# Two edits in a two-layer trunk kernel: the order of the second half's join at the inner norms, and the last held products in two halves of 256 columns

## The chip, the cores and the metric

The kernel runs on one core of one Trainium2 chip. The metric is the device time of one execution in microseconds; the time before is the median of three runs. Five engines work side by side and meet through semaphores: TensorE (PE in the profile, with its weight loads on a row of their own, PEld), VectorE (DVE), ScalarE (ACT), GpSimd (POOL) and SyncE (SP), which issues most DMAs. Each engine works through its own queue of instructions in order.

## The reference

The model has two layers over 256 tokens of 1024 features. Each layer is three steps, each followed by a layer norm over the features:

```python
for l in range(DEPTH):
    h = _swiglu(x, ffn_w1[l, 0], ffn_w3[l, 0], ffn_w2[l, 0])
    x = _layernorm(ALPHA * x + 0.5 * h, ln_g[l, 0], ln_b[l, 0])
    h = _mixer(x, l, ...)
    x = _layernorm(ALPHA * x + h, ln_g[l, 1], ln_b[l, 1])
    h = _swiglu(x, ffn_w1[l, 1], ffn_w3[l, 1], ffn_w2[l, 1])
    x = _layernorm(ALPHA * x + 0.5 * h, ln_g[l, 2], ln_b[l, 2])
return x
```

`_swiglu` is `(silu(x @ w1) * (x @ w3)) @ w2` with 2816 hidden features. `_mixer` projects x to seven parts, runs a gated spatial unit and a differential attention on them, merges both with sigmoid gates and multiplies by `w_out`. `_layernorm` subtracts the mean, divides by the root of the variance plus a small constant, and applies a gain and a bias. All data are float32.

## The kernel before, in words

**Products in three terms.** Every float32 operand of a large product is split into a hi part (the value rounded to the fast float32 format) and a lo part (the rest). A product is three: hi by hi, hi by lo and lo by hi (`three`, line 271). The hi parts are made by ScalarE, the lo parts by VectorE, which subtracts. For weights that is `stream` (lines 174 and 178) or, for the pieces that are loaded ahead of a norm, `ahead` and `rest_of` (207, 216, 227, 229). For activations it is `split` (233 for hi, 234 for lo). Weights are loaded by SP as `raw` tiles of 1 MB through a ring of four.

**Tokens in two row tiles.** The 256 tokens are two tiles of 128, t = 0 and t = 1. At the end of a step a row tile lies with its tokens on the partitions and its 1024 features in two halves of 512 columns; `x_tok[t]` holds it. The next step wants x with the features on the partitions, so it has to be turned.

**The inner norms (class `Norm`).** There are five: three behind an FFN and two behind a mixer. For each row tile, `part_s` (545) adds a half's products and sums the rows. `finish_s` takes the mean (551), then the sum of squares on ScalarE (553), the reciprocal root by three Newton steps on VectorE (`rsqrt`, 243 to 249), and the normalized rows (556), the second 512 columns first. `send` puts these second 512 columns into two planes of 16 bits (184) and has a DMA turn them (`turning`, 189). `turned` is a task that calls `turn(t, 0)` and `turn(t, 1)` after set numbers of beats; a beat is a count of products that TensorE has been given.

- `turn(t, 0)`: TensorE transposes the first 512 columns (633) into a bank; ScalarE applies gain and bias in four pieces of 128 (638), and `split` makes the hi part (ScalarE, 233) and the lo part (VectorE, 234).
- `turn(t, 1)`: ScalarE joins the two planes that the DMA has turned (628, "the join"); then 638, 233 and 234 as before.

The `part_s` of row tile 1 is queued behind the lo part of row tile 0's first half where that has been traced already.

**What sets the order.** TensorE's instructions stand in the order in which they are traced. On the other engines a scheduler at compile time sets each queue's order, by priority and by the times that it reckons. `soon()` gives the instructions in it a higher priority; `behind(ins)` puts each instruction traced in it behind `ins` in the queue of the engine that both use, and does nothing if `ins` is None. The join is in a `soon()` and has no `behind`.

**After a norm.** `gemm_b2` multiplies the turned x by the next weights, first for row tile 0 and then for row tile 1. For row tile 0 the first 512 columns (four blocks of 128) meet two matrices with three products each, and then the second 512.

**The end of an FFN.** `ffn` makes its last product in several pieces: products by a seven-product scheme (S banks), "plain pairs", and the last four pairs of blocks, which are held (`HELD` = 4) until the rest is done. The held products go bank by bank: for t and the column half c, 4 x 2 x 3 = 24 products 512 columns wide into `ends[t, c]`. For the last norm of the kernel, `part` then adds the bank to the rows (567), takes statistics in groups of 256 columns (572) and, at row tile 1, multiplies a part that does not reach the last column by the gain (574). At (t, c) = (1, 1) it is called twice, for 256 columns each, after the last of the 24 products. `finish` gathers the statistics (579), takes the root (583), has TensorE bring the first 768 columns of row tile 1 into banks and subtract the mean times the gain (588 and 592), ends the rows (594 to 600) and stores them in three cuts (601).

Of the kernel before, what the change touches and what calls it, by code (L numbers as in the profile page):

```python
# [17 lines left out]
ALU = mybir.AluOpType  # L18
# [4 lines left out]
T = 256  # L23
NT = T // P
# [9 lines left out]
PQ = [(k, k + 1) for k in (0, 2, *range(FB + 2 * NS, FT, 2))]  # L34
HELD = 4
# [23 lines left out]
def trunk(ctx, tc, x, xT, w13a, w13b, w2s, w2p, wb, wqk, wa, wbr, wo, gateb, sgug, sgub, sguwT, sgubias, lam, diffg,  # L59
          lng, lnb, lngT, lnbT, cosT, sinT, out):  # L60
    nc = tc.nc
    V, A, G, PE = nc.vector, nc.scalar, nc.gpsimd, nc.tensor
# [19 lines left out]
    def bank():  # L82
        return psum.tile([P, 512], F32, tag="main", name=name("bank"))
# [34 lines left out]
    @contextmanager  # L118
    def soon():
        was = tc.cur_priority  # L120
        tc.cur_priority = max(0, was - 2 * STEP)
        yield
        tc.cur_priority = was
# [27 lines left out]
    def behind(ins):  # L151

        return tc.issue_after(ins) if ins is not None else nullcontext()
# [158 lines left out]
    def rows_p(ps, t, q, piece, xh, xl, c0=0, n=512, stop=False, start=False):  # L312

        for j, k in enumerate(q):
            wh, wl = (v[:, j * 512 + c0 : j * 512 + c0 + n] for v in piece)
            three(ps[:, :n], xh(k)[:, t * P : (t + 1) * P], xl(k)[:, t * P : (t + 1) * P], wh, wl,
                  start and j == 0, stop and j == 1)
        beat(n / 1024)
# [190 lines left out]
    class Norm:  # L509
# [5 lines left out]

        def __init__(self, l, i, scale, eps, after, last=False):
            self.scale, self.eps, self.last, self.done = scale, eps, last, set()
            self.ends, self.xlo, self.pre, self.sent = [None] * NT, {}, None, {}
            self.gT, self.bT = (v[:, l, i] for v in (ln_g, ln_b))
            self.y = x_tok  # L520
            self.group = 256 if last else 512
            self.st = [sm("st", D // self.group * 6, bufs=2) for _ in range(NT)]
            self.g, self.b = bc_load(lng[l, i], after), bc_load(lnb[l, i], after)
            if last:
                A.activation(self.g, self.g, AF.Copy, scale=-0.5)
                self.minus = s512("minus")
                A.activation(self.minus[:, :P], ident, AF.Copy, scale=-1.0)
                self.eps_t = self.minus[:, 2 * P : 2 * P + 1]
                V.memset(self.eps_t, eps)
                with behind(silu[0]):  # L530
                    A.activation(sm("first", 1), mask[:, :1], AF.Sqrt)
            else:
                self.x = [xs.tile([P, 4, 512], F32R, tag="x", name=name("x")) for _ in range(2)]
# [88 lines left out]
        def turn(self, t, h):  # L622
            self.done.add((t, h))
            xf = s512("xf")
            if h:
                b = xf
                with soon():
                    A.activation(xf.bitcast(U16).rearrange("p (k w) -> p k w", w=2),
                                 self.sent[t].rearrange("p (w k) -> p k w", w=2), AF.Copy)
            else:  # L630
                b = side_bank()
                for k in range(4):
                    PE.transpose(b[:, k * P : (k + 1) * P], self.y[t][:, k * P : (k + 1) * P], ident)
            hi, lo = (self.x[h][:, :, o + t * P : o + (t + 1) * P] for o in (0, T))
            with soon(), behind(early[0] if t == 0 else None):
                for k in range(4):
                    s, f = slice(k * P, (k + 1) * P), slice(h * 4 + k, h * 4 + k + 1)
                    A.activation(xf[:, s], b[:, s], AF.Identity, scale=self.gT[:, f], bias=self.bT[:, f])  # L638
                with behind((None, self.ends[1])[h] if t == 0 else None):
                    last = split(hi, lo, xf.rearrange("p (k t) -> p k t", k=4))  # L640
            self.xlo[t, h] = last[1]
            if (t, h) == (1, 1):
                latest[:] = last

# [6 lines left out]
    def ffn(l, f, i, norm, following=None):  # L651
# [108 lines left out]
            ln.pre = ahead(following)  # L760
        for t in range(NT):
            for c in range(2):
                for ps, o, n in ends[t, c]:
                    for q in PQ[-HELD:]:
                        rows_p(ps, t, q, held[q, c], hh, hl, o, n, stop=q == PQ[-1])
                    if not last:
                        ln.part_s(t, c, ps)
                        continue
                    for o in ((0, 256) if last and (t, c) == (1, 1) else (0,)):
                        ln.part(t, c * 512 + o, ps[:, o : o + 256] if o or last and (t, c) == (1, 1) else ps, 1.0)  # L770
            (ln.finish if last else ln.finish_s)(t, ((2, 1.5), (2, 1))[t])
            if t == 0:
                with behind(ln.ends[0]):
                    ln.more(1, 0, S[7], ALU.subtract, ln.scale)
                    ln.more(1, 0, u, ALU.add)
                    ln.more(1, 1, v, ALU.add, ln.scale)
                    ln.more(1, 1, S[7], ALU.add)
# [323 lines left out]
```

## Time and profile before

| what | value |
|---|---|
| median of three runs | 1212.53 us (1212.32 to 1212.62) |
| the profiled execution's own time | 1213.05 us |
| its span, from the first to the last instruction | 1211.3 us |
| TensorE's share of the chain that ended last | 91% |
| VectorE's and ScalarE's shares of that chain | 4% and 3% |
| mean granted clock of TensorE | 1.000 |

In the timeline each row has the start and the duration in us, the engine, the line, the operation, the tiles written and read, and in brackets how long the engine had been idle and what ended that. Several instructions in a row of one kind are merged, with their count behind an x. In the list of waits the columns are the total, the number of waits and the longest. The chain that ended last has start, duration and what ran.

### The profile page before, as it was taken

What the parts mean: (1) busy time and instruction counts of PE and PEld (TensorE: products, weight loads), DVE (VectorE), ACT (ScalarE), POOL (GpSimd) and SP (SyncE); (2) the same over time, 40 slices, a digit from 0 to 9 for tenths busy, and PEclk for the clock granted to TensorE, in tenths of its full rate; (3) what the DMA queues carried; (4) which work ended last, traced back from release to release, by engine and by line L of the source; (5) the groups of instructions that cost most, each with busy time, mean ns of one, the idle gap of its engine ahead of it and who ended that gap; (6) DMA issues with size and microseconds to landing.
All of it is one profiled execution on the core that took longest, in us unless ns stands there. A gap on an engine that the chain in (4) does not pass through costs nothing.

```text
span 1211.3 us, 16542 instructions
## 1 busy us (share of the span) xinstructions
PE 1203.7 (99%) x5961; PEld 1011.3 (83%) x5961; DVE 942.9 (78%) x1540; ACT 857.4 (71%) x1384; POOL 91.1 (8%) x184
## 2 busy tenths in 40 slices
PE   9999999999999999999999999999999999999998
PEld 8888888888888878888888888888888888888886
DVE  6658998885696876579985679989766877757797
ACT  7677677679865595776776776776898556867761
POOL 0100000233300000000000000003331000000000
PEclk9999999999999999999999999999999999999999
DMA  8985665655764658665668665766648456677551
GB/s 321 323 261 174 211 249 208 227 177 166 232 227 164 217 178 282 191 192 218 229 216 270 195 176 207 254 223 199 213 139 273 176 174 217 201 259 210 184 202 47
DMA packets 101346, 257.00 MB, mean 212 GB/s; under 512 B 66528, under 2 KB 67600, under 8 KB 74640
## 3 DMA queue, kind: packets, MB, share of 16 engines
q1 hardware_dynamic: 97296, 243.03, 59.9%
q0 software_dynamic: 3536, 12.13, 3.2%
q8 instruction: 46, 0.75, 0.3%
q10 hardware_dynamic: 432, 0.79, 0.2%
q14 instruction: 36, 0.29, 0.1%
HBM read 235.47 MB, written 1.05 MB: 195 GB/s over the span
## 4 chain that ended last, share of the span: by engine, by line
PE 91%; DVE 4%; ACT 3%; issue 1%; DMA 0%; SPq 0%; POOL 0%; DVEq 0%; ACTq 0%; POOLq 0%
PE bank L271 35%; PE sbank L271 24%; PE bank L283 16%; PE bank L290 8%; PE sbank L283 2%; PE bank L446 2%; PE sbank L290 1%; PE sbank L829 1%; DVE wlo L178 1%; PE sbank L961 1%; ACT pp L839 0%; DVE nwa L248 0%; ACT xf L638 0%; ACT whi L174 0%; PE sbank L878 0%
## 5 line engine op out<-in xcount | busy, mean ns | idle before, releaser
L178 DVE TENSOR_TENSOR wlo<-raw,whi 128x1024 fp32r<-128x1024 f32 (+1 forms) x396 | 436.6, 1125 | 144.5 <-ACT whi L174 113.9
L174 ACT ACTIVATE whi<-raw 128x1024 fp32r<-128x1024 f32 (+1 forms) x396 | 372.9, 971 | 124.4 <-PE bank L283 43.2
L271 PE MATMUL bank<-whi,x 128*128 128x512 f32 x840 | 263.3, 390 | 0.0
L271 PEld LDWEIGHTS bank<-whi,x 128*128 128x128 f32 x840 | 157.7, 188 | 32.9 <-DVE gz L293 0.2
L271 PE MATMUL bank<-wlo,x 128*128 128x512 f32 x420 | 163.5, 389 | 0.0
L271 PE MATMUL sbank<-whi,x 128*128 128x512 f32 x512 | 158.9, 389 | 0.0
L283 PE MATMUL bank<-x,whi 128*128 128x512 f32 x640 | 156.0, 394 | 0.0
L283 PEld LDWEIGHTS bank<-x,whi 128*128 128x128 f32 x640 | 117.1, 188 | 26.3 <-issue 2.3
L271 PEld LDWEIGHTS sbank<-whi,x 128*128 128x128 f32 x512 | 96.1, 188 | 20.0
L353 ACT ACTIVATE shi<-raw 128x1024 fp32r<-128x1024 f32 (+1 forms) x80 | 73.4, 946 | 51.7 <-DVE raw L368 26.4
L271 PE MATMUL sbank<-wlo,x 128*128 128x512 f32 x256 | 99.6, 389 | 0.0
L355 DVE TENSOR_TENSOR slo<-raw,shi 128x1024 fp32r<-128x1024 f32 (+1 forms) x80 | 85.4, 1088 | 14.1 <-ACT shi L353 13.3
L271 PEld LDWEIGHTS bank<-wlo,x 128*128 128x128 f32 x420 | 78.9, 188 | 16.0
L290 PE MATMUL bank<-x,wlo 128*128 128x256 f32 x640 | 85.9, 285 | 0.0
L290 PEld LDWEIGHTS bank<-x,wlo 128*128 128x128 f32 x640 | 81.6, 191 | 2.2
L291 ACT ACTIVATE r<-bank 128x256 f32<-128x256 f32 x112 | 41.6, 377 | 24.0 <-PE bank L290 24.0
L271 PEld LDWEIGHTS sbank<-wlo,x 128*128 128x128 f32 x256 | 48.1, 188 | 9.9
L271 PE MATMUL sbank<-whi,hhi 128*128 128x512 f32 x144 | 56.3, 391 | 0.0
L271 PE MATMUL sbank<-whi,hlo 128*128 128x512 f32 x144 | 56.1, 390 | 0.0
L271 PE MATMUL sbank<-wlo,hhi 128*128 128x512 f32 x144 | 56.0, 389 | 0.0
L506 POOL DMA_DIRECT2D bc<-in_lng x6 | 3.2, 530 | 696.2 <-DVE bc L505 696.2
L702 ACT ACTIVATE planes<-silu 128x1024 uint16<-128x1024 uint16 x40 | 42.0, 1053 | 7.3 <-DVE silu L701 6.2
(247 smaller groups left out, 1999.1 us busy)
## 6 DMA issues: line engine op xcount, KB each, us to landing
raw<-in_w13b SPq DMA_DIRECT2D x76, 1024.0 KB, 5.4
raw<-in_w2p SPq DMA_DIRECT2D x24, 1024.0 KB, 4.9
raw<-in_wa SPq DMA_DIRECT2D x24, 1024.0 KB, 5.4
raw<-in_w2s SPq DMA_DIRECT2D x20, 1024.0 KB, 4.9
raw<-in_wb SPq DMA_DIRECT2D x16, 1024.0 KB, 5.3
raw<-in_wqk SPq DMA_DIRECT2D x16, 1024.0 KB, 4.8
raw<-in_wbr SPq DMA_DIRECT2D x16, 1024.0 KB, 4.9
raw<-in_w13a SPq DMA_DIRECT2D x8, 1024.0 KB, 4.8
```

The source lines that it names most:

```text
L174: copied = A.activation(h, r, AF.Copy)
L178: V.tensor_tensor(out=w, in0=r, in1=h.bitcast(F32), op=ALU.subtract)
L271: PE.matmul(ps, xx, w, start=start and n == 0, stop=stop and n == 2)
L283: PE.matmul(b[-1], hi[:, k * P : (k + 1) * P], xc(k), start=k == 0, stop=False)
L290: PE.matmul(b[n][:, :T], lo[:, k * P : (k + 1) * P], xc(k)[:, :T], start=False, stop=k == KT - 1)
L291: emptied[0] = A.activation(r[:, s], b[n][:, T:], AF.Copy, scale=scale).ins
L353: A.activation(h, r, AF.Copy)
L355: V.tensor_tensor(out=w, in0=r, in1=h.bitcast(F32), op=ALU.subtract)
L446: PE.matmul(ps[t][m], x[:, j, o + t * P : o + (t + 1) * P], y, start=k0 + j == 0 and o == 0 and y is hi, stop=k0 + j == KT - 1 and y is lo)
L702: A.activation(pk.rearrange("p (w k) -> p w k", w=2), s.bitcast(U16).rearrange("p (k w) -> p w k", w=2), AF.Copy)
L829: PE.matmul(banks[m][:, j * nk : (j + 1) * nk], rows(qT, m, j, t * P, P), rows(kT, m, j, 0, nk), start=True, stop=True)
L961: PE.matmul(b[:, j * T + t * P : j * T + (t + 1) * P], vg[t][:, g // 4, s], wsT[g // 4][:, s], start=True, stop=True)
```

## The change

At row tile t the hi part's instruction of `turn(t, 0)` is kept in `xhi[t]`, and the join of `turn(t, 1)` is queued behind it on ScalarE. At the last norm, for (t, c) = (1, 1) alone, the held products are done in two halves. The 24 of the left half write columns 0 to 255 of the bank that also holds the sums so far of all 512 columns. Then `part` is called for them, and the old sums in the bank's columns 256 to 511 are added to the rows. The 24 of the right half go to a new bank, which they start from nothing, and `part` adds that to the rows. For all other t and c the products and calls stay what they were.

```diff
             self.scale, self.eps, self.last, self.done = scale, eps, last, set()
-            self.ends, self.xlo, self.pre, self.sent = [None] * NT, {}, None, {}
+            self.ends, self.xlo, self.pre, self.sent, self.xhi = [None] * NT, {}, None, {}, {}
...
             xf = s512("xf")
             if h:
                 b = xf
-                with soon():
+                with soon(), behind(self.xhi[t]):
                     A.activation(xf.bitcast(U16).rearrange("p (k w) -> p k w", w=2),
                                  self.sent[t].rearrange("p (w k) -> p k w", w=2), AF.Copy)
...
                     last = split(hi, lo, xf.rearrange("p (k t) -> p k t", k=4))
-            self.xlo[t, h] = last[1]
+            self.xhi[t], self.xlo[t, h] = last
...
         for t in range(NT):
             for c in range(2):
-                for ps, o, n in ends[t, c]:
-                    for q in PQ[-HELD:]:
-                        rows_p(ps, t, q, held[q, c], hh, hl, o, n, stop=q == PQ[-1])
-                    if not last:
-                        ln.part_s(t, c, ps)
-                        continue
-                    for o in ((0, 256) if last and (t, c) == (1, 1) else (0,)):
-                        ln.part(t, c * 512 + o, ps[:, o : o + 256] if o or last and (t, c) == (1, 1) else ps, 1.0)
+                (ps, _, _), = ends[t, c]
+                if last and (t, c) == (1, 1):
+                    y, right = ln.y[t][:, 768:], bank()
+                    for b, o, opens in ((ps, 0, False), (right, 256, True)):
+                        for q in PQ[-HELD:]:
+                            rows_p(b[:, :T], t, q, held[q, c], hh, hl, o, 256, stop=q == PQ[-1],
+                                   start=opens and q == PQ[-HELD])
+                        ln.part(t, 512 + o, b[:, :T], 1.0)
+                        if not opens:
+                            V.tensor_tensor(out=y, in0=y, in1=ps[:, T:], op=ALU.add)
+                    continue
+                for q in PQ[-HELD:]:
+                    rows_p(ps, t, q, held[q, c], hh, hl, 0, 512, stop=q == PQ[-1])
+                if last:
+                    ln.part(t, c * 512, ps, 1.0)
+                else:
+                    ln.part_s(t, c, ps)
```

## The prediction

> **What bounds the kernel now.** First the head of the page. Its first row has the span, and the row of busy times says how much of it is not matrix products.
>
> ```profile
> span 1211.3 us, 16542 instructions
> ```
> ```profile
> PE 1203.7 (99%) x5961; PEld 1011.3 (83%) x5961; DVE 942.9 (78%) x1540; ACT 857.4 (71%) x1384; POOL 91.1 (8%) x184
> ```
>
> TensorE (PE) is busy for 1203.7 of 1211.3 us. An edit that takes no products away can only win back holes between them and the tail behind the last one. So the second view is the list of waits, for TensorE alone. Two of its rows belong to the inner norms:
>
> ```profile
> PE sbank L633 <- DVE xtok L556: 0.8, 2, 0.4
> PE bank L271 <- DVE x L234: 0.5, 3, 0.2
> ```
>
> L234 writes the lo part of the turned x, which the next layer multiplies by. L556 writes the normalized rows, which TensorE transposes at L633. The idle times listed are smaller than the holes in the order of starts, so I measured the holes there. There are two kinds of norm: three follow an FFN, two a mixer. I show one of each; the others of a kind repeat them to some hundredths. Behind an FFN, in the timeline, ScalarE (ACT) first:
>
> ```profile
> 780.44 1.19 ACT L628 ACTIVATE xf<-sent 128x1024 uint16<-128x1024 uint16 x1
> 781.51 0.64 ACT L233 ACTIVATE x<-xf 128x512 fp32r<-128x512 f32 x1
> 782.04 1.65 ACT L638 ACTIVATE xf<-xf,ln_b,ln_g 128x128 f32<-128x128 f32 x4
> 783.58 0.63 ACT L174 ACTIVATE whi<-raw 128x512 fp32r<-128x512 f32 x1
> 784.10 0.63 ACT L233 ACTIVATE x<-xf 128x512 fp32r<-128x512 f32 x1
> 784.62 1.14 ACT L553 ACTIVATE sq<-xtok,mv 128x1024 bf16<-128x1024 f32 x1
> ```
>
> L628 at 780.44 is the join of the second 512 columns of row tile 0. It stands ahead of L233 at 781.51, the hi part of the first 512 columns, which TensorE needs first. VectorE (DVE) in the same stretch:
>
> ```profile
> 781.77 0.69 DVE L178 TENSOR_TENSOR wlo<-raw,whi 128x512 fp32r<-128x512 f32 x1
> 782.37 0.69 DVE L234 TENSOR_TENSOR x<-xf,x 128x512 fp32r<-128x512 f32 x1
> 782.98 0.69 DVE L545 SCALAR_TENSOR_TENSOR xtok<-xtok,sbank 128x512 f32<-128x512 f32 x1
> ```
>
> And TensorE:
>
> ```profile
> 782.31 0.40 PE L271 MATMUL bank<-lhi,x 128*128 128x512 f32 x1
> ...
> 783.12 0.73 PE L271 MATMUL bank<-lhi,x 128*128 128x512 f32 x2 [0.18 <-DVE x L234]
> 783.70 0.39 PE L271 MATMUL bank<-llo,x 128*128 128x512 f32 x1
> ```
> The pace of products 512 and then 256 columns wide, from the chain of work that ended last:
>
> ```profile
> 1113.77 21.76 PE bank L271 x96
> ```
> ```profile
> 1142.78 3.83 PE sbank L290 x32
> ```
>
> That is 226.7 ns for a wide and 119.7 ns for a narrow one. The fifth product of the new layer should start 4 x 0.227 us after the first, at 783.22. It starts at 783.70, so the hole is 0.48 us: the third product needs the lo part, which ends at 783.06.
>
> Behind a mixer (ScalarE, VectorE, TensorE):
>
> ```profile
> 424.38 1.18 ACT L628 ACTIVATE xf<-sent 128x1024 uint16<-128x1024 uint16 x1
> 425.46 0.63 ACT L233 ACTIVATE x<-xf 128x512 fp32r<-128x512 f32 x1
> ```
> ```profile
> 426.12 0.69 DVE L234 TENSOR_TENSOR x<-xf,x 128x512 fp32r<-128x512 f32 x1 [2.05 <-ACT x L233]
> ```
> ```profile
> 426.14 0.50 PE L271 MATMUL bank<-lhi,x 128*128 128x512 f32 x1
> ...
> 427.44 0.39 PE L271 MATMUL bank<-llo,x 128*128 128x512 f32 x1
> ```
>
> The fifth product is due at 427.05 and starts at 427.44: a hole of 0.39 us. A second hole follows where the transposes of row tile 1 wait for L556, 0.39 us as listed:
>
> ```profile
> 433.89 0.66 PE L633 MATMUL sbank<-ident,xtok 128*128 128x128 f32 x4 [0.39 <-DVE xtok L556]
> ```
>
> **Part 1, the join behind the hi part.** Nothing is added or removed; at row tile 0 of five norms L628 goes behind L233. At row tile 1 the hi part already runs first. Only ScalarE's order is constrained; the transposing DMA is issued by SP ahead of the join and is not moved.
>
> What is queued behind the join is L638 and the hi part of the second 512 columns. Swapping two instructions moves neither, as the ScalarE work in front of them stays the same: they still start at 782.04 and after. Their products come 24 places after 782.31 (the first 512 columns are four blocks of 128, by two matrices, by three products), at 782.31 + 24 x 0.227 = 787.75, and that hi part ends at 784.73. So this costs nothing: the cover is 3.0 us, and still 1.9 if L553 (1.14 us) gets ahead of it, as below.
>
> What is won is how much earlier the hi part runs. At most this is the join's step, 781.51 - 780.44 = 1.07 us. At least it is about half. The compile-time scheduler sets ScalarE's order, and at 783.58 it put a weight cast (L174) between L638 and the second hi part, evidently because it reckoned that L638's result was not there yet. Where the join stood it will probably put that cast, 0.52 us from start to start (783.58 to 784.10). The hi part would then start at 780.96 instead of 781.51 and end at 781.60; in the mixers it starts at 424.90.
>
> Can VectorE follow? Behind an FFN it has no gap, so the lo part must be put one place ahead of the L178 at 781.77. It would then end at 782.46, and TensorE wants it at 782.31 + 2 x 0.227 = 782.76. Behind a mixer VectorE is idle, and the lo part follows at once. So the holes of 0.48 and 0.39 us close in either case.
>
> **What is late next.** TensorE now reaches the transposes of row tile 1 (L633) earlier, and these end a chain of their own: lo part, L545, L551, L553 on ScalarE, the reciprocal root, L556. Behind an FFN its end and the transposes' first weight load are
>
> ```profile
> 788.17 1.00 DVE L556 TENSOR_SCALAR xtok<-xtok,mv,nwy 128x512 f32<-128x512 f32 x2
> ```
> ```profile
> 789.38 0.59 PEld L633 LDWEIGHTS sbank<-ident,xtok 128*128 128x128 f32 x4
> ```
>
> so L556 ends at 789.17, with 0.21 us of slack. Behind a mixer there is none. If that chain stays where it is, an FFN norm wins 0.21 us and a mixer norm nothing.
>
> Does it move? L551, which L553 needs, stands in the two kinds at
>
> ```profile
> 784.18 0.22 DVE L551 TENSOR_SCALAR mv<-st 128x1 f32<-128x1 f32 x1
> ```
> ```profile
> 428.06 0.21 DVE L551 TENSOR_SCALAR mv<-st 128x1 f32<-128x1 f32 x1
> ```
>
> L553 starts at 784.62 because L174 and L233 had gone ahead of it while L551 was not ready. L551 stands behind L545, and that behind the lo part. With the lo part one place (0.60 us) earlier, L551 starts at 783.58 and ends at 783.80. ScalarE, with the cast already done, is through L638 at about 784.10, again with the second hi part reckoned not ready. This time L553 can fill that place: 784.10 instead of 784.62, 0.52 us earlier. Behind a mixer, likewise, the lo part comes 0.56 us earlier (424.90 against 425.46) and L551 ends near 428.27 - 0.56 = 427.71. ScalarE's order there is
>
> ```profile
> 427.52 0.63 ACT L174 ACTIVATE whi<-raw 128x512 fp32r<-128x512 f32 x1
> ```
> ```profile
> 428.56 1.14 ACT L553 ACTIVATE sq<-xtok,mv 128x1024 bf16<-128x1024 f32 x1
> ```
>
> so with the cast already done it is free at 428.04 = 427.52 + 0.52, and L553 again moves 0.52 us. Then an FFN norm gets its whole 0.48 us and a mixer norm 0.52 us. Bounds: FFN 0 to 0.48, mixer 0 to 0.39 + 0.39 = 0.78 (both holes, for which the chain would have to move by that much).
>
> Sum of the likeliest: 3 x 0.48 + 2 x 0.52 = 2.48 us.
>
> **Part 2, the two halves.** Instead of 24 products of 512 columns there are 48 of 256. By the two rows of the chain they take 48 x 119.7 = 5.75 us instead of 24 x 226.7 = 5.44 us: 0.31 us more, and on the path, since TensorE is continuous there. From below the cost can hardly be under zero, as the columns are the same in number; above, it is a rival. [...]
>
> The tail behind the last product is where it pays back:
>
> ```profile
> 1203.13 0.75 DVE L567 TENSOR_TENSOR xtok<-xtok,sbank 128x256 f32<-128x256 f32 x2 [2.38 <-PE sbank L271]
> 1203.80 0.74 DVE L572 BATCH_NORM_STATS2 st<-xtok 128x6 f32<-128x256 f32 x2
> 1204.46 0.41 DVE L574 TENSOR_TENSOR xtok<-xtok,bc 128x256 f32<-128x256 f32 x1
> 1204.78 0.26 DVE L579 BATCH_NORM_AGGREGATE mv<-st 128x2 f32<-128x24 f32 x1
> 1205.07 0.51 DVE L594 SCALAR_TENSOR_TENSOR xtok<-xtok,mv,bc 128x256 f32<-128x256 f32 x1
> ```
>
> Five instructions stand between the last product and L579, 1204.78 - 1203.13 = 1.65 us. Afterwards only two do: one L567 and one L572. The left half's L567, L572, L574 and the added sum of the old right columns, at about 0.41 each by L574's row, 1.6 us, lie in the time of the right half's products, 24 x 119.7 = 2.87 us. VectorE is idle there: 2.38 us by the first row. If that cover were gone, they would stand in the tail as now, plus one add.
>
> The two that remain depend on each other, so each waits for the end of the one before; L594 starts 0.03 after L579's end (1204.78 + 0.26). So 2 x (0.41 + 0.04) = 0.90 us, a saving of 0.75. Run as close as now, 0.33 us apart, they would take 0.66 and save 0.99. I take 0.75. All that follows, to the output, shifts with L579. Net: 0.75 - 0.31 = 0.44 us won, between 0.2 and 0.7. The new bank costs nothing that the profile would show: it is one of the main banks, of which the first was emptied long before.
>
> **Sum.** 2.48 + 0.44 = 2.92 us. The profiled execution took 1213.05 us, 1.75 beyond its span, and 0.52 above the median of the three runs, 1212.53. I subtract from both: 1210.1 profiled, 1209.6 as a median.
>
> **The rivals.**
>
> 1. The row-tile-1 chain stays (L553 not moved): 3 x 0.21 + 0 + 0.44 = 1.07 us, 1211.5. For it: at 784.10 ScalarE takes the hi part, which is wanted too. Against it: the scheduler filled that place with a mere cast. 0.24.
> 2. The hi part gains the whole step and the chain goes with it: 3 x 0.48 + 2 x 0.78 + 0.44 = 3.44 us, 1209.1. For it: a cast may be lacking where the join stood. Against it: L174 was there to be taken at 427.52. 0.12.
> 3. Part 1 does nothing: casts fill ScalarE ahead of the hi part, or VectorE leaves the lo part where it is. Then only 0.44, 1212.1. Against it: VectorE had idled 2.05 us for just this hi part at 426.12. 0.08.
> 4. Slower. The halves double the weight loads, 24 more. If they are exposed, each costs up to the duration in this row:
>
> ```profile
> L271 PEld LDWEIGHTS bank<-whi,x 128*128 128x128 f32 x840 | 157.7, 188 | 32.9 <-DVE gz L293 0.2
> ```
>
> That is 24 x 0.188 = 4.51 us in place of 0.31; with 2.48 and 0.75 won it ends at +1.3 us, 1213.8. It decides from (2.48 + 0.75) / 24 = 135 ns of each load. Against it stand the 32 narrow products in 3.83 us: 119.7 ns each, loads included. 0.03. [...]
>
> **How the numbers follow.** The forecast has 0.52, and 0.01 is left for a loss from elsewhere in the reordered queues. About 0.2% (2.4 us) is what a measurement of this kernel can tell from no change. The forecast, 2.92, lies 0.5 beyond; its own uncertainty (0.3 in the tail, about 0.5 in the two mixer norms) leaves some three quarters of its cases over, 0.39. With rival 2 that is 0.51 for faster. Rivals 1 and 3, most of 4 and the rest of the forecast lie within, 0.47; 0.02 is slower. The range 1208.6 to 1211.7 takes in rivals 1 and 2, with half a microsecond below rival 2 for the tail's bound and for idle times that the list gives too small, and leaves out 3 and 4.
>
> **What would show it.** ScalarE: L233 ahead of L628 at row tile 0, with or without an L174 between. TensorE: the fifth product 0.91 us after the first; the first L633 of row tile 1 waiting or not. L553 ahead of the second hi part is the forecast; behind it, rival 1. Tail: products 119.7 ns apart, and L579 0.9 us behind the last one. Wrong would be holes that move to L633 or to the second 512 columns of row tile 1, or narrow products slower than 130 ns.

## The result and the profile after

The changed kernel takes 1215.39 us (median of 15 runs, 1213.96 to 1216.14), the kernel before on the same chip 1212.95 us (15 runs, 1212.30 to 1213.84). The ratio is 1.0018, with a 95% interval of 1.0010 to 1.0026: it is slower, by 2.4 us, where 2.9 us less was forecast. Below, "profiled" always means the one profiled execution of a kernel; the changed kernel's took 1214.40 us against 1213.05 before, 1.35 us more. The other 1.1 us between profile and median are taken up under the last experiments. A ratio is not quite the quotient of the two medians (they differ by up to 0.0005 below), and an interval belongs to its ratio. Two single executions further down, one of edge_into_ffn and one of changed_again, took over twice the time of the others; the medians count them, the ratios and the spreads do not.

The head of the page and the list of waits of TensorE, of the changed kernel:

```profile
span 1212.6 us, 16586 instructions
...
PE 1203.4 (99%) x5985; PEld 1013.7 (84%) x5985; DVE 943.4 (78%) x1541; ACT 857.9 (71%) x1384; POOL 91.5 (8%) x184
```
```profile
PE sbank L838 <- ACT aT L874: 1.6, 2, 1.1
PE sbank L633 <- DVE xtok L556: 1.5, 2, 0.8
...
PE sbank L592 <- ACT minus L590: 0.7, 1, 0.7
```

TensorE is busy for the same time, 1203.4 us against 1203.7, so what was lost is waits. The row `x L234` of the kernel before is gone, `xtok L556` has grown from 0.8 to 1.5 us, and the first row was not in the list at all: L838 (L829 before; lines from 771 on have moved by nine) makes the scores of the attention, and waits for L874, which copies transposed probabilities out of a bank. No step of the forecast had looked there.

To place the difference I matched TensorE's instructions of the two traces one by one and took the difference of their starts. It is flat over long stretches and steps at a few places:

| place (its time in the kernel before) | step, us |
|---|---|
| three norms behind an FFN (183, 605, 783) | -0.23, -0.24, -0.21 |
| two norms behind a mixer (426, 1026) | +0.02, +0.01 |
| attention of layer 1 (273.02) | +1.00 |
| attention of layer 2 (871.93 to 872.68), and its gated spatial unit (947.5) | +1.16, +0.21 |
| held products and tail of the last norm (1197 to 1206) | +0.29, then -0.73 |

The steps make -0.68 + 0.03 + 2.37 - 0.44 = +1.28 us; the spans differ by 1.3.

**The norms.** Behind an FFN, ScalarE and then TensorE:

```profile
781.01 0.64 ACT L174 ACTIVATE whi<-raw 128x512 fp32r<-128x512 f32 x1
781.53 0.64 ACT L233 ACTIVATE x<-xf 128x512 fp32r<-128x512 f32 x1
782.05 1.20 ACT L628 ACTIVATE xf<-sent 128x1024 uint16<-128x1024 uint16 x1
...
784.97 0.63 ACT L233 ACTIVATE x<-xf 128x512 fp32r<-128x512 f32 x1
785.51 1.13 ACT L553 ACTIVATE sq<-xtok,mv 128x1024 bf16<-128x1024 f32 x1
```
```profile
782.88 0.39 PE L271 MATMUL bank<-lhi,x 128*128 128x512 f32 x1
...
783.78 0.39 PE L271 MATMUL bank<-llo,x 128*128 128x512 f32 x1
...
789.45 0.39 PE L271 MATMUL bank<-whi,x 128*128 128x512 f32 x1
789.96 0.66 PE L633 MATMUL sbank<-ident,xtok 128*128 128x128 f32 x4
```

The cast L174 stands where the join stood, then the hi part, then the join. The fifth product starts 0.90 us after the first: the hole of 0.48 is closed. But L553 stands behind the second hi part, so the transposes L633 come 0.51 us after the product before them, where 0.23 is the step of one product. The hole has moved there, and 0.21 of it is won, by the table.

Behind a mixer, ScalarE and TensorE:

```profile
426.21 1.20 ACT L628 ACTIVATE xf<-sent 128x1024 uint16<-128x1024 uint16 x1
427.29 0.64 ACT L174 ACTIVATE whi<-raw 128x512 fp32r<-128x512 f32 x1
...
429.35 1.15 ACT L553 ACTIVATE sq<-xtok,mv 128x1024 bf16<-128x1024 f32 x1
```
```profile
434.69 0.66 PE L633 MATMUL sbank<-ident,xtok 128*128 128x128 f32 x4 [0.76 <-DVE xtok L556]
```

Here L553 does stand ahead of the second hi part, but a second cast (427.29) has come in behind the join. TensorE's wait at L633 grows from 0.39 to 0.76 us, by what the first hole gave.

**The tail.** VectorE and TensorE of the changed kernel:

```profile
1205.14 0.42 DVE L567 TENSOR_TENSOR xtok<-xtok,bank 128x256 f32<-128x256 f32 x1 [1.33 <-PE bank L271]
1205.60 0.43 DVE L572 BATCH_NORM_STATS2 st<-xtok 128x6 f32<-128x256 f32 x1
1206.06 0.26 DVE L579 BATCH_NORM_AGGREGATE mv<-st 128x2 f32<-128x24 f32 x1
```
```profile
1204.70 0.28 PE L271 MATMUL bank<-wlo,hhi 128*128 128x256 f32 x1
1204.82 0.28 PE L271 MATMUL bank<-whi,hlo 128*128 128x256 f32 x1
1204.94 1.45 PE L588 MATMUL sbank<-xtok,ident 128*128 128x512 f32 x4
1207.06 1.56 PE L592 MATMUL sbank<-bc,minus 128*128 128x512 f32 x4 [0.66 <-ACT minus L590]
```

Two instructions instead of five stand between the last product and L579, 1206.06 - 1205.14 = 0.92 us, and the narrow products start 0.12 us apart.

**The attention.** In the kernel before, the scores (PE) and the order on VectorE around them were:

```profile
272.22 1.94 PE L829 MATMUL sbank<-qk,qk 64*128 64x256 f32 x8
```
```profile
267.99 1.40 DVE L848 SCALAR_TENSOR_TENSOR pp<-pp,c,pp 128x256 f32<-128x256 f32 x4
269.31 0.68 DVE L809 TENSOR_TENSOR qk<-qk,swap 128x512 f32<-128x512 f32 x1
```

and in the changed kernel:

```profile
272.00 0.70 PE L838 MATMUL sbank<-qk,qk 64*128 64x256 f32 x2
273.80 1.13 PE L838 MATMUL sbank<-qk,qk 64*128 64x256 f32 x6 [1.10 <-ACT aT L874]
```
```profile
267.20 0.69 DVE L818 TENSOR_TENSOR qk<-qk,swap 128x512 f32<-128x512 f32 x1 [1.46 <-POOL swap L814]
267.82 0.21 DVE L865 SCALAR_TENSOR_TENSOR c<-rc,neg_lam,sums 128x4 f32<-128x4 f32 x1
...
268.34 1.40 DVE L857 SCALAR_TENSOR_TENSOR pp<-pp,c,pp 128x256 f32<-128x256 f32 x4
```

L818 is the last rotary sum (L809 before) and L857 the difference of probabilities (L848 before). Their order has turned round. The rotary sum needs GpSimd's product of L814, so VectorE stands idle for 1.46 us, with L857 behind it. The chain of waits of the changed kernel shows how this reaches TensorE (start, duration, what ran):

```profile
265.88 1.30 POOL swap L814
...
267.20 0.69 DVE qk L818
...
268.34 1.40 DVE pp L857 x4
269.74 1.14 DVE wlo L178
270.88 0.34 DVE gz L293
...
271.66 0.38 ACT sbank L895 x2
272.04 0.95 ACT whi L174
272.98 0.28 ACT sbank L895 x2
273.27 0.49 ACT aT L874
...
273.80 1.13 PE sbank L838 x6
```

VectorE's part of this chain does not end late. Its last step, L293, ends at 271.22; in the same chain of the kernel before its last step is

```profile
271.04 0.43 DVE gz L293
```

which ends at 271.47, and TensorE is 0.22 us ahead in the changed kernel as well. The loss is made behind L293, on ScalarE, whose order has changed as well. Around the copy of L874 (L865 before) its queue has four squares (L895, L886 before), two gates (L933, L924 before) and one weight cast. In the kernel before, the cast stood behind the first square, ahead of both gates. In the changed kernel it (272.04 in the chain) stands behind both gates, and ScalarE waits for the second of them:

```profile
270.10 1.05 ACT L174 ACTIVATE whi<-raw 128x1024 fp32r<-128x1024 f32 x1
```
```profile
271.25 0.51 ACT L933 ACTIVATE gate<-gz,gbh 128x256 f32<-128x256 f32 x1 [0.61 <-DVE gz L293]
```

The cast's 0.95 us are now in the chain. The bank for the scores also comes free with L874, at 273.75; in the kernel before it came free with the last square, at 272.97, which ran ahead of the copy. The nearest edited line, the join of the norm ahead, ran some 80 us earlier. The diff changes no line of the mixer and adds no edge there; these queues are the work of the scheduler at compile time.

### The profile page after: what moved, and what is told of

Its sections match the earlier page's. It is cut to its first block, busy times and chain, and to the rows that moved or that the text cites. A ratio compares the mean times of both kernels' runs of the same rounds, so it can differ in the third digit from the quotient of the medians.

```text
span 1212.6 us, 16586 instructions
## 1 busy us (share of the span) xinstructions
PE 1203.4 (99%) x5985; PEld 1013.7 (84%) x5985; DVE 943.4 (78%) x1541; ACT 857.9 (71%) x1384; POOL 91.5 (8%) x184
## 4 chain that ended last, share of the span: by engine, by line
PE 89%; ACT 4%; DVE 4%; issue 1%; POOL 1%; DMA 0%; SPq 0%; DVEq 0%; ACTq 0%; POOLq 0%
PE bank L271 33%; PE sbank L271 23%; PE bank L283 16%; PE bank L290 8%; PE sbank L283 2%; PE bank L446 2%; PE sbank L290 1%; ACT xf L638 1%; ACT whi L174 1%; PE sbank L838 1%; DVE wlo L178 1%; DVE nwa L248 1%; PE sbank L970 1%; DVE xtok L556 1%; DVE nwy L249 1%
## 5 line engine op out<-in xcount | busy, mean ns | idle before, releaser
L178 DVE TENSOR_TENSOR wlo<-raw,whi 128x1024 fp32r<-128x1024 f32 (+1 forms) x396 | 438.4, 1129 | 149.6 <-ACT whi L174 120.6
L174 ACT ACTIVATE whi<-raw 128x1024 fp32r<-128x1024 f32 (+1 forms) x396 | 372.9, 971 | 124.0 <-PE bank L283 38.8
L283 PE MATMUL bank<-x,whi 128*128 128x512 f32 x640 | 156.0, 394 | 0.0
L283 PEld LDWEIGHTS bank<-x,whi 128*128 128x128 f32 x640 | 117.1, 188 | 26.3 <-issue 2.7
L271 PE MATMUL sbank<-whi,hhi 128*128 128x512 f32 (+1 forms) x144 | 55.5, 385 | 0.0
L271 PE MATMUL sbank<-whi,hlo 128*128 128x512 f32 (+1 forms) x144 | 55.2, 384 | 0.0
L271 PE MATMUL sbank<-wlo,hhi 128*128 128x512 f32 (+1 forms) x144 | 55.2, 383 | 0.0
```

What stands on the lines that cost most here:

```text
L174: copied = A.activation(h, r, AF.Copy)
L178: V.tensor_tensor(out=w, in0=r, in1=h.bitcast(F32), op=ALU.subtract)
L271: PE.matmul(ps, xx, w, start=start and n == 0, stop=stop and n == 2)
L283: PE.matmul(b[-1], hi[:, k * P : (k + 1) * P], xc(k), start=k == 0, stop=False)
```

## The experiments

Three theories stood after the two traces. **A:** the loss is the attention's rearrangement alone, and the scheduler made it because the plan ahead of it had shifted. **B:** the two halves of the tail cost time. **C:** the wait at L633 behind the mixers is the loss. Each kernel below was run 11 times and is compared with the kernel before on the same chip (21 to 33 runs; its medians were 1212.83, 1212.64, 1212.94 and 1212.76 us beside the four groups).

**halves_only**: the join as before, the two halves kept.

```diff
-                with soon(), behind(self.xhi[t]):
+                with soon():
```

> The second part alone: the last held products in two halves, the join as before. Theory A (the loss sits in the attention of both mixers, whose queues the compile-time scheduler has rearranged because of the join's new place; the halves themselves are a gain): 0.4 to 0.5 us faster than before, attention as before. Rival B (the narrow products, or the wait of L592 for L590 that is new in the tail, cost the time): 1.5 to 2.5 us slower than before.

Measured: 1212.44 us, 0.39 less than before, ratio 0.9997 (0.9988 to 1.0006). The attention has the order of the kernel before. B falls. The term of the tail, 0.44, agrees, but the interval takes in no change as well; what shows the term is the two steps of the table, +0.29 and -0.73.

**join_only**: the edge kept, the held products as before (the loop's added lines of the diff put back).

> The first part alone: the join behind the hi part at all five inner norms, the last products undivided. Theory A: 2.5 to 3.2 us slower than before, with the scores of one head pair (line 829 of the kernel before) waiting about 1 us for the copy at line 865 in each mixer. Rival B: no slower than before, 0.5 to 1.1 us faster.

Measured: 1215.08 us, 2.25 more than before, ratio 1.0020 (1.0011 to 1.0029). The profile has the same 1.6 us in two waits of L829 for L865. The loss comes with the edge.

**edge_into_ffn**: the edge only at norms that feed an FFN: both behind a mixer, and the one between the two layers. The halves kept.

```diff
-            self.y = x_tok
+            self.y, self.edge = x_tok, i > 0
...
-                with soon(), behind(self.xhi[t]):
+                with soon(), behind(self.xhi[t] if self.edge else None):
```

> Both parts, but the join is queued behind the hi part only at the three norms that feed an FFN (two behind a mixer, one behind an FFN); at the two that feed a mixer the order is the one before. Theory A: the attention's order and time are as before; what is left is 0.2 us at the FFN norm, about nothing at the two mixer norms and 0.44 us in the tail: 0.5 to 0.8 us faster than before. Rival C (the hole that moves to the transposes of row tile 1 behind a mixer is itself the loss, as it grew from 0.55 to 0.95 us): 1 us slower or more, attention or not.

Measured: 1212.23 us, 0.60 less than before, ratio 0.9993 (0.9984 to 1.0002). The wait at L633 is 1.5 us here as in the changed kernel, and yet there is no loss: C falls. The attention's queues are those of the kernel before.

**pin_rope_sum**: the changed kernel, with the last rotary sum held behind L857.

```diff
-                with behind(None if last else added[0]):
+                with behind(lessened[0] if last else added[0]):
...
-                    V.scalar_tensor_tensor(out=pp[0][:, s], ...
+                    lessened[0] = V.scalar_tensor_tensor(out=pp[0][:, s], ... ).ins
```

> The changed kernel, with one further edge: the rotary sum of the last k (line 818) is queued behind the last of the four combinations of the two softmaxes (line 857) that were traced before it, as it stood in the kernel before. The other rearrangements in the attention stay. Theory A, with this sum as the one that matters (VectorE waits there 1.4 us for GpSimd with the combinations behind it): the scores of line 838 wait no longer, and the kernel is 0.8 to 1.3 us faster than before. Theory A with the other rearrangements mattering too (the casts and gates on ScalarE): between that and the changed kernel. Rivals B and C: as slow as the changed kernel, 2.4 us over before.

Measured: 1213.26 us, 0.43 more than before, ratio 1.0004 (0.9995 to 1.0013). That takes back 2.0 of the 2.4 us, but not all that was expected of it: its wait for the copy is still 0.6 us in layer 1. The edge didn't act on L818 alone. On VectorE it also put one L293 back behind L857, and on ScalarE, against the changed kernel, the cast stands ahead of both gates again (270.17). So the run shows that this group of swaps makes most of the loss; by the chain above it is the cast's that TensorE feels. What is left is in others.

**pin_both**: pin_rope_sum, and one lo part of a gate piece, which had moved forward by ten places of VectorE's queue, held behind the last rotary product.

```diff
...
-                (_, b), = gemm_a2([wa[l, sec, c]], both, lambda m: t512("gz"), lambda: t512("r"))
+                (_, b), = gemm_a2([wa[l, sec, c]], both, lambda m: t512("gz"), lambda: t512("r"),
+                                  after=(None, roped[0] if (br, c) == (0, 3) else None))
```

> This is the changed kernel with two instructions of VectorE's queue fixed by hand where the kernel before has them: the last rotary sum (L818) stays behind the subtraction L857, and the lo part of one gate piece (the L178 that writes wlo_2869) stays behind the rotary product L813. With both, the attention has the kernel before's order on VectorE and ScalarE throughout; the join's new place and the two halves stay. Theory A (the loss is the rearranged attention and nothing else): the offsets at the attention vanish, and what is left is the first row tile's hole less 0.22 us at each of three FFN norms, nothing at the two mixer norms, 0.44 us at the end: 1.1 us faster than the kernel before, 1.4 at most, 0.8 at least. Rival D (the order is not what costs; the attention is slow because its transfers and GpSimd's steps meet VectorE's work at another moment, which any shift of the norm brings): attention still loses 0.9 us or more in the two layers, and the whole stays within 0.3 us of the kernel before or slower.

Measured: 1211.76 us, 0.88 less than before, ratio 0.9993 (0.9984 to 1.0002), near the 1.1 expected. With these two instructions held, VectorE's and ScalarE's queues in both mixers are those of the kernel before, but for one sum at the first head pair that stands one place earlier, and L838 is gone from the list of waits, which begins

```profile
PE sbank L633 <- DVE xtok L556: 1.6, 2, 0.8
```

So A holds, and rival D (the moment, not the order) falls. The interval alone would still let pass a time near that of the kernel before; it is the trace, with no wait left at L838, that decides. By their medians 3.3 us (2.44 + 0.88) lie between two kernels that differ in the order of queues alone.

**edge_into_mixer**: the complement of edge_into_ffn (`i == 0` in place of `i > 0`).

> The complement: the join edge only at the two FFN norms that feed a mixer, the two halves kept. Its attention has the changed kernel's order. Theory A: 2 x 0.22 and 0.44 us won, some 2.4 to 3.0 us lost in the attention of the two layers: 1.5 to 2.1 us slower than the kernel before, with TensorE waiting for the copy of the transposed probabilities (L865) 1.5 us or more in all. Rival: if the join's place at the other norms has a part in the loss, this one is less than 1 us slower.

Measured: 1215.83 us, 3.19 more than before, ratio 1.0021 (1.0012 to 1.0030). The direction is A's, the size is not: 1.1 us more than the upper end expected.

**late_casts_no_edge**: no edge anywhere, the halves, and a few weight casts at the norms queued behind L553.

```diff
...
-                with behind(latest[0] if o // HC in lent else early[0] or latest[0]):
+                with (behind(latest[0] if o // HC in lent else early[0] or latest[0]),
+                      behind(late[0] if (o, p) in late[1] else None)):
                     copied = A.activation(h, r, AF.Copy)
...
```

> No join edge at all (every join stands where the kernel before has it), the two halves kept, and only the few weight casts at the norms queued behind L553. VectorE's and ScalarE's queues in the attention then have the changed kernel's order, not the kernel before's, though nothing was changed within 80 us of it. Theory A in its general form (it is not the join edge that costs, but that any edit at a norm that feeds a mixer lets the scheduler settle on that other order): 0.44 us won at the end, 2.4 to 3.0 us lost in the attention, some 2 to 2.6 us slower than the kernel before. Rival: if the join's place has its own part in the attention's loss, this one stays within 1 us of the kernel before.

Measured: 1215.79 us, 2.85 more than before, ratio 1.0026 (1.0017 to 1.0035). VectorE's and ScalarE's queues in the mixers are the changed kernel's, instruction by instruction, without the changed kernel's edge. It is not the join that costs. Another edit at the same norms has tipped the scheduler into the same other order.

**pin_and_late_casts** and **late_casts_into_ffn**: the same edit of the casts, on top of pin_both and of edge_into_ffn. They were to open L553 the place that the forecast had given it.

> This is pin_both with the weight casts (L174) that had moved into the freed time ahead of row tile 1's square (L553) queued behind that square: two of them at a mixer norm, one at an FFN norm. Theory: the forecast's second step failed because a cast took the join's place ahead of L553. With the casts behind it L553 starts up to 1.0 us earlier at a mixer norm; its operand is written by L551 at 427.6 to 427.8 against its start at 428.09 in the kernel with edges only into an FFN, and L551 itself sits behind one lo part of 0.6 us that moves too, so 0.3 to 0.8 us are to be had; the wait at L633 falls from 0.75 to 0.1 to 0.5 us, and at FFN norms from 0.25 to nothing. In all 1.1 + 2 x 0.5 + 3 x 0.25 = 2.85 us faster than the kernel before, 2.0 at least. Rival E (L556 is held by VectorE's other work in the Newton chain, lo parts of 0.6 us that stand between its steps, not by L553): the waits at L633 stay as they were and the kernel is as fast as pin_both, 1.1 us faster than the kernel before.

> The join edge only at norms that feed an FFN (two mixer norms, one FFN norm), with the casts behind L553 as in pin_and_late_casts, so the attention is the kernel before's without any pin. The edge alone gave 0.60 us in this form. Theory of the casts: 0.60 + 2 x 0.5 + 0.25 = 1.85 us faster than the kernel before, between 1.2 and 2.3. Rival E: no more than 0.6 us faster, L633 still waits 0.75 us at both mixer norms.

Measured: 1212.24 us, 0.40 less than before, ratio 0.9994 (0.9986 to 1.0003); and 1212.71, 0.07 more, ratio 0.9999 (0.9991 to 1.0008). Both medians are higher than without the casts' edit, by 0.5 and 0.7 us, which the intervals can't tell from nothing; the traces say why they are not lower. The wait at L633 behind the mixers grew from 0.8 to 1.0 us. VectorE of pin_and_late_casts (its lines 174 to 386 have moved by one: L249 is the Newton step 248, L179 the lo part 178):

```profile
430.37 0.68 DVE L179 TENSOR_TENSOR wlo<-raw,whi 128x512 fp32r<-128x512 f32 x1
430.96 0.26 DVE L249 TENSOR_SCALAR nwa<-nwy,ve 128x1 f32<-128x1 f32 x1
431.15 0.68 DVE L179 TENSOR_TENSOR wlo<-raw,whi 128x512 fp32r<-128x512 f32 x1
...
431.88 0.68 DVE L179 TENSOR_TENSOR wlo<-raw,whi 128x512 fp32r<-128x512 f32 x1
```

The casts' lo parts came later with them, into the gaps of the Newton chain that leads to the normalization: three of 0.6 us each, where pin_both has one, beside a lo part of x that stands there in both. This was rival E; whether VectorE's order is what bounds row tile 1 behind a mixer, the next two runs say.

**lo_behind_normalize** and **pins_and_lo_behind**: the lo parts of one half piece held behind row tile 1's L556, at the two norms behind a mixer; on top of halves_only and of pin_both.

```diff
-            after[1:3] = [(norm.ends[0], norm.ends[0])] * 2
+            after[1:3] = (norm.ends[0],) * 2, (norm.ends[0], norm.ends[norm.pre is None])
```

> No join edge and no pin; the two halves; at the two mixer norms the two lo parts (L178) of the second half of one weight piece are queued behind row tile 1's L556, not between the Newton steps that lead to it. In the kernel before two such lo parts of 0.60 us each stand in that chain (it runs from 430.02 to 432.83, while at an FFN norm, with none, the same chain of the kernel with both pins runs from 186.54 to 188.40). Theory F (the second row tile's chain is set by VectorE's order, not by ScalarE's): the hole at L633 of 0.55 us at both mixer norms closes, 2 x 0.55 + 0.44 = 1.5 us faster than the kernel before, 1.0 at least. Rival G: the lo parts are then late for their products; TensorE waits at L271 for L178 instead, and it is as fast as the two halves alone, 0.4 us.

> pin_both and, at the two mixer norms, the lo parts behind L556 as in lo_behind_normalize. Theory F: the wait at L633 (0.8 us at each mixer norm in pin_both) falls by 0.6 us at each: 1.1 + 2 x 0.6 = 2.3 us faster than the kernel before, 1.7 at least. If it holds, the forecast's 2.9 us were there to be had, but for the attention's order and for VectorE's lo parts in the chain. Rival G: TensorE waits at L271 for the late lo parts, and it is no faster than pin_both (1.1 us by its span's difference, 0.9 by its median).

Measured: 1211.37 us, 1.57 less than before, ratio 0.9987 (0.9978 to 0.9996); and 1211.05, 1.89 less, ratio 0.9988 (0.9979 to 0.9997). Theory F holds, and VectorE's order it is: TensorE's list of waits has no row for L633 in the first, and 0.6 us in two waits in the second (1.6 in pin_both). No wait for a lo part took its place, so G falls. The second has the lowest median of the study, 0.4 us short of what was expected of it; some 0.6 us are left at L633. Whether it is faster than the first, 0.3 us by the medians, can't be told from these intervals.

**hole_filled** and **changed_again**. One thing stayed open. The steps in the mixers explain some 2.4 us in the profile of the changed kernel. The medians ask for up to 4: edge_into_mixer lost 3.19 us in all, though 0.2 at each of two norms and 0.44 in the tail should have been won. The times of the changed kernel lie in two groups, 1214.0 to 1214.9 (7 of 15) and 1215.4 to 1216.1. In the profile of edge_into_mixer, which took 1216.14 us, the table of stretches has one reason (the column behind POOL's is the granted clock):

```profile
272.00:274.00 2.00, 0.86 (x4) 0.45 (x6) 1.09 (x1) 2.00 (x7) 0.00 (x0) 1.00 0.72 270
274.00:276.00 2.00, 2.00 (x10) 1.40 (x7) 1.12 (x3) 2.00 (x5) 1.58 (x6) 0.78 0.49 205
276.00:278.00 2.00, 2.00 (x6) 1.22 (x4) 2.00 (x9) 1.05 (x5) 1.59 (x6) 0.50 0.40 57
278.00:280.00 2.00, 2.00 (x13) 1.55 (x13) 1.30 (x12) 2.00 (x10) 1.01 (x5) 0.87 0.75 287
```

In the changed kernel's profile, with the same wait, the clock stays at 1.00:

```profile
276.00:278.00 2.00, 2.00 (x15) 1.39 (x14) 2.00 (x7) 1.01 (x4) 1.67 (x5) 1.00 0.37 53
```

The eight products of L283 that run through the fall take 3.48 us (from 274.75), against 2.11 in the changed kernel (from 274.86). I tried to take TensorE's pause away by dummy products in it, which nothing uses, and ran the changed kernel once more beside it.

```diff
+                if hp == HEADS // 2 - 1 and t == 1:
+                    for _ in range((5, 2)[l]):
+                        PE.matmul(banks[0], x_cat[0][:, 0, :P], x_cat[0][:, 0], start=True, stop=True)
```

> The changed kernel with dummy products (512 columns, x by x, 227 ns each, written to the bank that the next products start anew) ahead of the first products of the last head pair's scores: five in layer 1, two in layer 2, about as long as TensorE's waits there of 1.10 and 0.46 us. They compute nothing that is used. ScalarE's queue is as late as in the changed kernel; only TensorE's pause is filled. Theory H (a pause of 1.1 us there lets the granted clock fall to 0.50 for some 3 us, in some executions and not in others, and that is why the median of the changed kernel lies 1.0 us above its profiled execution): the pause is gone, the granted clock stays at 1.00, the times gather where the lower half of the changed kernel's lie: lowest about the same, highest some 1 us lower, median 0.5 to 1.0 us lower. Rival I (the spread comes from elsewhere): same median within 0.3 us and the same spread of 2 us.

> The changed kernel as it is, on the same chip as hole_filled, for the spread of its times and a second profiled execution. Theory H: the times fall in two groups about 1.2 us apart, 1214.0 to 1214.9 and 1215.3 to 1216.2, with the median 2.0 to 2.8 us above the kernel before; if the profiled execution is of the upper group its granted clock falls to 0.50 at about 275 us or 874 us, if of the lower group it stays at 1.00. Rival I: one broad group, and a profiled execution above 1215.3 us with a clock of 1.00 throughout.

Measured: hole_filled 1215.33 us, 2.57 more than before, ratio 1.0022 (1.0013 to 1.0031); changed_again 1214.84, 2.08 more, ratio 1.0018 (1.0009 to 1.0027). Of what theory H expects, the pause is gone in hole_filled, its clock stays at 1.00 in all the stretches of both attentions, and its spread is 1215.2 to 1216.2 against 1214.0 to 1216.8. But the median is 0.5 us higher, not lower. Its TensorE starts are level with changed_again's behind the scores of layer 1 and lose 1.7 us later, in steps of 0.1 to 0.7 us from 307 us on: the dummies have shifted the scheduler's plan as well, and casts stand elsewhere. So the run doesn't isolate the clock. changed_again's profiled execution took 1213.96 us, of the lower group, with a clock of 1.00, as H has it; its times, seven from 1214.0 to 1215.0 and three from 1215.8 to 1216.8, part less clearly than H had them. Shown is that the clock fell to 0.50 behind this pause in two of the five profiled executions that have it, and cost about 1.4 us in edge_into_mixer (the difference of its starts against halves_only's grows from 1.44 to 2.81 us while it lasts). For the group, the mean granted clock on record for each execution says something. Where a trace shows the fall, it is 0.998. That value stands beside 15 executions, all of kernels with this pause and all of 1215.63 us or more, four of them in the changed kernel's upper group of eight; no execution of a kernel without the pause has it. But 1215.72 us, in the same group, stands beside 1.000, and the 3.4 us at half that can be estimated from edge_into_mixer's stretches (0.88 + 2.00 + 0.52) would have taken 0.0014 off. So the clock likely makes a part of the upper group and doesn't make all of it; what makes the rest stays open.

## Why the prediction was wrong, step by step

- **The step that failed** is the cost of the swap: "Swapping two instructions moves neither, as the ScalarE work in front of them stays the same", "So this costs nothing", and 0.01 "for a loss from elsewhere in the reordered queues". At the norm itself the cover held. What was not reckoned is that `behind` is an input to a scheduler which plans all that follows by reckoned times. The edge changed the plan at the norms that feed a mixer, and VectorE's and ScalarE's queues came out differently 80 us further on, in a stretch where TensorE has no slack: 2.37 us in the profile where the forecast had 0, about 3.3 in the medians (changed kernel against pin_both, each against its own baseline: 2.44 + 0.88). The prediction had used the scheduler's freedom three times, always in its own favour, at the norm: a cast fills the join's place, the lo part moves up, L553 moves up. It did not ask what the same freedom would do elsewhere. That an edit's plan can tip far away is shown by late_casts_no_edge and both pins; why the scheduler then prefers that order stays open.
- **Rival 4**, the slower one, put the loss in the weight loads of the narrow products. It alone had the sign right, at +1.3 us, and by luck: the mechanism was not there. The narrow products start 0.12 us apart as the rows of the chain had it.
- **"The hi part would then start" half a step earlier, a cast in the join's place, the lo part one place up:** right at all five norms. The holes of 0.48 and 0.39 us closed.
- **"This time L553 can fill that place"** failed. Behind an FFN the second hi part was taken first, behind a mixer a second cast. What is late next was named rightly and came as in rival 1: 0.23, 0.24 and 0.21 us won behind an FFN (0.21 there), nothing behind a mixer. Of the 2.48 us of part 1 that leaves 0.68. The runs with late casts show more: even with ScalarE's place free, the lo parts in VectorE's Newton chain hold L556, which neither forecast nor rival had priced.
- **The halves:** 0.29 us more of TensorE (0.31 forecast), 0.73 saved behind it (0.75), 0.44 net; 0.39 in the median of halves_only. L592 now waits 0.66 us for ScalarE's L590, but stands as far behind L579 as before (1207.06 - 1206.06 = 1.00 us; 1205.77 - 1204.78 = 0.99 before).
- **The rest of the sum:** rival 1's 1.07 us is what the two edits bring by themselves. pin_both, which is the changed kernel with the mixer's order kept, gained 0.88 by its median, and the steps of the table outside the mixers make 1.09.
- **"About 0.2% (2.4 us) is what a measurement of this kernel can tell from no change"** was too wide. With 15 executions of each kernel the interval is 0.0008 on either side, 1.0 us, so a loss of 2.4 us is told clearly.

## What to carry to other kernels

Where a scheduler orders the queues at compile time, the cost of an ordering edge is not read at the edge alone: compare the queues of the two compiled kernels over their whole length, and count the stretch behind the edit as at risk wherever TensorE waits on a tight chain. A new order that hurts can be taken back by holding one or two instructions where they stood; find them by the first instruction that waits where it did not wait before. And when a chain of tiny dependent steps is late, look for wide work of the same engine in its gaps before moving other engines' work out of its way.

## What the runs showed of the hardware

**Behind two of six pauses of 1.1 us the granted clock fell to 0.50.** Five profiled executions have in all six pauses of TensorE of 1.10 to 1.15 us in the attention. Behind two of them (edge_into_mixer and late_casts_no_edge, both in layer 1) the granted clock fell to 0.50; behind the other four it stayed at 1.00. An estimate from the means of edge_into_mixer's stretches (0.78, 0.50 and 0.87 in 2 us each), with the clock taken as either 1.00 or 0.50: it fell near 275.12, some 1.4 us after the work had resumed at 273.69, and for some 3.4 us. What sets the two apart was not found.

**Three instructions of VectorE and GpSimd took 1.0 us longer beside one of the other engine.** VectorE and GpSimd in the kernel before, and GpSimd in the changed kernel, have

```profile
265.71 1.22 DVE L856 SCALAR_TENSOR_TENSOR c<-rc,neg_lam,sums 128x4 f32<-128x4 f32 x1
```
```profile
265.62 1.30 POOL L805 TENSOR_TENSOR swap<-swap,sin_t 128x512 f32<-128x512 f32 x1
```
```profile
264.12 1.19 POOL L262 TENSOR_TENSOR nwa<-nwa,ve 128x4 f32<-128x4 f32 x1
```

L856 took 0.21 us in the changed kernel (L865, 267.82 above), and L262 takes 0.20 at the median of its 24. Each lay beside a long two-input instruction of the other engine and ended with it, to 0.06 us: GpSimd's product L805 ran from 265.62 to 266.92 in the kernel before, and VectorE's L178 from 264.02 to 265.25 in the changed one. The lo part that pin_both holds back took 2.23 us in the changed kernel (257.75), beside GpSimd's product of 257.61 to 258.90, and 1.22 in the kernel before. So L856 took 1.01 us more, L262 0.99 and the lo part 1.01. Why, no run shows.
